# The up products of a gated decoder block: one wide and one narrow matmul per k, and weight sums held behind the up unit's low parts

## The chip, the core and the metric

The kernel runs on one core of one Trainium2 chip. The metric is the time of the program on the device in microseconds (us); lower is better. The engines are TensorE (PE; PEld are its weight loads), VectorE (DVE), ScalarE (ACT), GpSimd (POOL) and SyncE (SP). Each takes its own instructions in the order in which they were built; they meet at semaphores only.

## What is computed

One decoder block on 256 tokens of width 2048, in float32: a mixing half (mLSTM and block attention, merged by gates), then a squared-ReLU MLP with 8192 hidden channels. The change lies in the MLP:

```python
hn = rmsnorm(x, norm_ffn_pre[l])
u = jnp.square(jax.nn.relu(jnp.einsum('bsd,df->bsf', hn, w_up[l])))
y = jnp.einsum('bsf,fd->bsd', u, w_down[l])
x = x + rmsnorm(y, norm_ffn_post[l])
```

## The kernel before

**Products in three parts.** Every float32 operand is split into a high part (rounded to the matmul's input type, by a ScalarE cast, line 167, tiles `whi`) and a low part (what is left, by a VectorE subtraction, line 170, tiles `wlo`). A product is hi x hi + hi x lo + lo x hi. The moving tile of a k holds both parts of the activations side by side, 256 tokens each.

**Two forms of the product by channels.** `mm_feat` (lines 193 and 194), used by the projections, takes two matmuls per k: the high weights against both parts, 512 columns into a whole accumulator, and the low weights against the high part, 256 columns into its first half. `both` (lines 243 and 245) then brings the second half out with a ScalarE copy and adds it to the first on VectorE. `mm_feat_one` (lines 220 to 222) takes three matmuls of 256 columns, all into the first half, and needs no such addition; the up products use it.

**Weight units.** A weight unit is 128 x 2048 (1 MB), loaded by SP into a `raw` tile (3 buffers) or a `rawl` tile (4), and split in two halves of 1024 columns into `whi` and `wlo` (4 buffers each, so two units). An up unit makes 128 of the hidden channels, with 16 k. Its result goes through `up_post`: VectorE takes the maximum with 0 and multiplies by the norm's row factor `rbc` (line 770), ScalarE squares (line 775).

**Chunks.** The MLP runs in 8 chunks of 1024 hidden channels. The down products of chunks 0 to 6 use a seven-product scheme for 2 x 2 blocks in place of eight products. A chunk has two groups p = 0, 1 of seven products, in the order p1, q5, p6, p2, q7, q3, q4. Their weights are the blocks b11, b21, b22 and sums of blocks:

- the weight of q5, `t` = b11 + b12, made on VectorE by the *first sum* (line 879) while b11's unit is prepared; after it, a POOL-queue DMA adds b22 onto b12 (line 880), for q7
- the weight of p6, `t` + b22, made by the *second sum* (line 887) after the split of q5's weight; after the split of that, another POOL-queue DMA adds b21 (line 894), for q4

The activations' factors are sums too (`factors`, lines 787 to 814), made at a chunk's start. Between the down products D of a chunk stand the eight up units U of the next one, as `DUDUDDUDUDDUDUDDUDUDDD`; the second group starts with the eighth D.

**What sets the order.** A loop over the steps emits step i's load and split, then what lies in the list `behind`, then the matmuls and the post of step i - 1. From this program order a scheduler builds each engine's queue; it may move instructions, but `keep_in_program_order` pins those that it is given. A queue does not change at run time. Where L770 stands ahead of a split on VectorE, that split waits until the up unit is done.

Of the kernel before, what the change touches and what calls it, by code (L numbers as in the profile page):

```python
# [19 lines left out]
ALU = mybir.AluOpType  # L20
# [4 lines left out]
T = 256  # L25
# [60 lines left out]
def tile_hybrid_block(ctx, tc, xT, pos, pre, small, wa, wi, wo, wu, wd, wpost, out):  # L86
    nc = tc.nc
    V, S, G, PE = nc.vector, nc.scalar, nc.gpsimd, nc.tensor
# [14 lines left out]
    def t256():  # L103
        return tmp.tile([P, T], F32, name="t256", tag="t256", bufs=6)
# [16 lines left out]
    rbc = const.tile([P, T], F32, name="rbc")  # L121
# [118 lines left out]
    def both(acc):  # L240

        b = t256()
        S.copy(out=b, in_=acc[:, T:2 * T])
        s = t256()
        V.tensor_tensor(out=s, in0=acc[:, 0:T], in1=b, op=ALU.add)
        return s
# [295 lines left out]
    def feat_step(src, mov, post, after_k=None, tail=0, product=mm_feat):  # L542
        st = {}

        def mm(units):
            st["a"] = [acc_tile() for _ in units]
            product(st["a"], units, mov, after_k=after_k, tail=tail)
        steps.append((src if isinstance(src, list) else [src], mm, lambda: post(*st["a"])))
# [217 lines left out]
    uh, xs, todo, behind = {}, {}, [], []  # L766

    def up_post(j, i, acc):
        r = t256()
        V.scalar_tensor_tensor(out=r, in0=acc[:, 0:T], scalar=0.0, in1=rbc, op0=ALU.max,  # L770
                               op1=ALU.mult)
        c = i // 4
        if i % 4 == 0:
            uh[c] = pool["f"].tile([P, 4, T], F32, name="u", tag="u", bufs=2)
        S.activation(out=uh[c][:, i % 4], in_=r, func=AF.Square)
        if j < NCH - 1 and i == 7:
            todo.extend(factors(j))
            for _ in range(2):
                todo.pop(0)()
        elif j == NCH - 1 and i % 4 == 3:  # L780
            for h in range(2):
                factor((j, c, h), uh[c][:, :, h * P:(h + 1) * P])
# [75 lines left out]
    def group(j, p):  # L858
# [5 lines left out]
        r, acc = {}, {}  # L864
# [10 lines left out]
        def w_b11():  # L875
            r["11"], r["12"], r["t"] = load(b11), long_raw(), long_raw()
            nc.sync.dma_start(out=r["12"], in_=b12)
            parts = split(r["11"])
            V.tensor_tensor(out=r["t"], in0=r["11"], in1=r["12"], op=ALU.add)
            nc.gpsimd.dma_start(out=r["12"], in_=b22, accum_op=ALU.add)  # L880
            return [parts]

        def w_t1():
            r["22"] = long_raw()
            nc.sync.dma_start(out=r["22"], in_=b22)
            parts = split(r["t"])
            V.tensor_tensor(out=r["t"], in0=r["t"], in1=r["22"], op=ALU.add)
            return [parts]

        def w_t2():  # L890
# [138 lines left out]
        steps.append(([wd[8 * j + 6], wd[8 * j + 7]], mm, post))  # L1029

    def up_step(j, i):
        feat_step(wu[8 * j + i], hmov, lambda a: up_post(j, i, a), product=mm_feat_one)

    def down_group(j, p):

# [2 lines left out]
        def part(n, what):  # L1038
            def f(*a):
# [8 lines left out]

    feat_step([wu[c] for c in range(4)], hmov, first_up, after_k=x1_squares, tail=4,
              product=mm_feat_one)
    for i in range(4, 8):
        up_step(0, i)
    for j in range(NCH - 1):
# [38 lines left out]
    for i in range(len(steps) + 1):  # L1094
        if i < len(steps) and i not in units:
            src = steps[i][0]
            if i < 4:
                if i == 3:
                    nc.sync.dma_start(out=sm_in, in_=small)
                raws[i] = raw_tile()  # L1100
                start_load(i, raws[i])
                units[i] = [split(raws.pop(i), pieces=2,
                                   between=lambda q, i=i: split_x(4 * i + q))]
            elif callable(src):
                units[i] = src()
            elif len(src) < 4:
                place = places[i]() if i in places else None
                units[i] = [split(load(s), place, half=s.shape[1] // 2, pinned=i in places)
                            for s in src]
            else:  # L1110

                extra = [split(load(s), p.tile([P, 2, 2, 1024], F32R, name=n, tag=n))
                         for s, p, n in ((src[2], pool["mg"], "wu2"), (src[3], pa, "hm"))]
                units[i] = [split(load(src[0]))]

                raw1 = load(src[1])
                late["square"]()
                u1 = [split_half(raw1, 0, pinned=True)]
                late["then"] = lambda: u1.append(split_half(raw1, 1, pinned=True))
                run_step(i - 1)  # L1120
                units[i] += [u1] + extra
                residual()

                raw = load(steps[i + 1][0][0])
                units[i + 1] = [[split_half(raw, 0)]]
                late["then"] = lambda: units[i + 1][0].append(split_half(raw, 1, pinned=True))
                run_step(i)
                continue
            while behind:
                behind.pop(0)()  # L1130
        if i and i - 1 in units:
            run_step(i - 1)
# [71 lines left out]
```

## Time and profile before

| | |
|---|---|
| median of 3 runs | 1424.61 us (1424.54 to 1424.98) |
| profiled execution: its time / its span | 1423.46 / 1421.7 us |
| TensorE busy | 1407.6 us, 99% |
| VectorE busy | 1106.7 us, 78% |
| ScalarE busy | 813.9 us, 57% |
| granted TensorE clock, mean | 0.998 of full speed |

The profile was taken from one execution. Busy time of TensorE is modelled at its ends, since matmuls overlap: the distance from one start to the next tells how fast they run. A row "x2" stands for two instructions merged; "idle before" and the name behind the arrow say how long the engine waited just before and what ended the wait. The MLP takes the last 700 us of the span.

### The profile page before, as it was taken

Reading aid. Unit: us, or ns where it says so; the run is one execution under the profiler, and the core shown is the slowest. Engines: PE = TensorE matmul, PEld = TensorE weight load, DVE = VectorE, ACT = ScalarE, POOL = GpSimd, SP = SyncE. Lnnn points to the kernel's source line nnn. Section 1 sums busy time; section 2 is a strip of 40 time slices with the busy share of each in tenths; the row PEclk is TensorE's granted clock in tenths of the full one; section 3 lists DMA queues with packets and bytes.
Section 4 is the critical chain, followed back from the end, with each engine's and each line's share of the span. In section 5 each row is a group of like instructions: output and inputs, shape, how many; then the busy total and the mean of one; then the engine's idle time right before and its main releaser. Section 6 shows DMA issues by size and latency. Waiting matters only on the chain.

```text
span 1421.7 us, 21825 instructions
## 1 busy us (share of the span) xinstructions
PE 1407.6 (99%) x8570; PEld 1252.6 (88%) x8570; DVE 1106.7 (78%) x1571; ACT 813.9 (57%) x1200; POOL 29.4 (2%) x45
## 2 busy tenths in 40 slices
PE   9999999999999999999999999999999999999997
PEld 7888888888888888888899989989889899988885
DVE  7777766777676666665687888898888989889985
ACT  7655555565554454455656666565655655666561
POOL 0000000000000000000000000000000000000000
PEclk9999999999999999999999999999999999999999
DMA  8654444455445555555618776878768778776761
GB/s 261 221 184 175 159 175 184 177 184 178 178 178 180 192 192 179 191 193 178 238 62 296 250 224 235 269 239 289 232 193 290 234 244 263 239 233 240 242 232 60
DMA packets 46471, 297.13 MB, mean 209 GB/s; under 512 B 5340, under 2 KB 7648, under 8 KB 11936
## 3 DMA queue, kind: packets, MB, share of 16 engines
q1 hardware_dynamic: 41904, 265.57, 49.9%
q0 software_dynamic: 4320, 30.15, 11.4%
q8 instruction: 67, 1.10, 0.3%
q14 instruction: 36, 0.29, 0.1%
q10 hardware_dynamic: 144, 0.01, 0.0%
HBM read 293.61 MB, written 2.10 MB: 208 GB/s over the span
## 4 chain that ended last, share of the span: by engine, by line
PE 96%; DVE 1%; DMA 1%; ACT 0%; issue 0%; SPq 0%; DVEq 0%; ACTq 0%
PE acc L193 27%; PE acc L194 14%; PE acc L222 9%; PE acc L221 9%; PE acc L220 9%; PE acc L231 6%; PE acc L237 6%; PE acc L235 6%; PE acc L205 2%; PE acc L210 2%; PE acc L209 2%; PE sm L231 1%; PE sm L237 1%; PE sm L235 1%; DMA raw<-in_wa_dram 1%; DVE wlo L170 1%
## 5 line engine op out<-in xcount | busy, mean ns | idle before, releaser
L170 DVE TENSOR_TENSOR wlo<-raw,whi 128x1024 fp32r<-128x1024 f32 (+2 forms) x420 | 493.5, 1183 | 218.8 <-ACT whi L167 208.9
L167 ACT CAST whi<-raw 128x1024 fp32r<-128x1024 f32 (+2 forms) x420 | 424.9, 1017 | 406.2 <-PE acc L193 173.8
L193 PE MATMUL acc<-xw,whi 128*128 128x512 f32 x1152 | 408.4, 395 | 0.0
L194 PE MATMUL acc<-xw,wlo 128*128 128x256 f32 x1152 | 328.6, 285 | 0.0
L222 PE MATMUL acc<-hw,wlo 128*128 128x256 f32 x992 | 279.7, 282 | 1.3 <-DVE wlo L170 1.1
L221 PE MATMUL acc<-hw,whi 128*128 128x256 f32 x992 | 279.4, 282 | 0.0
L220 PE MATMUL acc<-hw,whi 128*128 128x256 f32 x992 | 277.7, 282 | 0.0
L193 PEld LDWEIGHTS acc<-xw,whi 128*128 128x128 f32 x1152 | 216.4, 188 | 48.9 <-issue 0.4
L167 ACT CAST whi<-rawl 128x1024 fp32r<-128x1024 f32 x168 | 173.5, 1047 | 113.1 <-PE acc L221 59.0
L194 PEld LDWEIGHTS acc<-xw,wlo 128*128 128x128 f32 x1152 | 216.6, 188 | 0.9
L170 DVE TENSOR_TENSOR wlo<-rawl,whi 128x1024 fp32r<-128x1024 f32 x168 | 201.3, 1221 | 7.0 <-ACT whi L167 5.4
L222 PEld LDWEIGHTS acc<-hw,wlo 128*128 128x128 f32 x992 | 187.1, 189 | 5.3 <-DVE wlo L170 2.9
L220 PEld LDWEIGHTS acc<-hw,whi 128*128 128x128 f32 x992 | 185.9, 188 | 4.2
L221 PEld LDWEIGHTS acc<-hw,whi 128*128 128x128 f32 x992 | 186.8, 188 | 2.1
L231 PE MATMUL acc<-whi,xs 128*128 128x512 f32 x356 | 141.0, 396 | 0.0
L235 PE MATMUL acc<-whi,xs 128*128 128x512 f32 x356 | 140.8, 395 | 0.0
L237 PE MATMUL acc<-wlo,xs 128*128 128x512 f32 x356 | 138.8, 395 | 0.0
L193 PE MATMUL acc<-mg,whi 128*128 128x512 f32 x240 | 84.2, 393 | 0.0
L235 PEld LDWEIGHTS acc<-whi,xs 128*128 128x128 f32 x356 | 66.9, 188 | 14.6
L231 PEld LDWEIGHTS acc<-whi,xs 128*128 128x128 f32 x356 | 66.8, 188 | 13.9 <-ACT whi L167 1.4
L237 PEld LDWEIGHTS acc<-wlo,xs 128*128 128x128 f32 x356 | 66.9, 188 | 13.9
L194 PE MATMUL acc<-mg,wlo 128*128 128x256 f32 x240 | 67.7, 283 | 0.0
(266 smaller groups left out, 1732.3 us busy)
## 6 DMA issues: line engine op xcount, KB each, us to landing
raw<-in_wi_dram SPq DMA_DIRECT2D x96, 1024.0 KB, 4.8
raw<-in_wu_dram SPq DMA_DIRECT2D x64, 1024.0 KB, 7.4
rawl<-in_wd_dram SPq DMA_DIRECT2D x42, 1024.0 KB, 8.9
rawl<-in_wd_dram POOLq DMA_DIRECT2D x28, 1024.0 KB, 9.3
raw<-in_wd_dram SPq DMA_DIRECT2D x22, 1024.0 KB, 7.1
raw<-in_wo_dram SPq DMA_DIRECT2D x16, 1024.0 KB, 4.8
raw<-in_wa_dram SPq DMA_DIRECT2D x8, 520.0 KB, 5.0
raw<-in_wa_dram SPq DMA_DIRECT2D x16, 256.0 KB, 5.2
```

The costliest lines, as they stand in the source:

```text
L167: first = S.copy(out=hi[:, s], in_=r)
L170: second = V.tensor_tensor(out=lo[:, s], in0=r, in1=hi[:, s].bitcast(F32), op=ALU.subtract)
L193: PE.matmul(out=accs[i][:, 0:2 * T], lhsT=hi, rhs=m, start=k == 0, stop=False)
L194: PE.matmul(out=accs[i][:, 0:T], lhsT=lo, rhs=m[:, 0, :], start=False, stop=k == nk - 1)
L205: first = PE.matmul(out=acc, lhsT=m[:, 0, ts], rhs=hi, start=start and k == 0, stop=False)
L209: PE.matmul(out=acc, lhsT=m[:, 1, ts], rhs=hi, start=False, stop=False)
L220: PE.matmul(out=acc, lhsT=hi, rhs=m[:, 0, :], start=k == 0, stop=False)
L221: PE.matmul(out=acc, lhsT=hi, rhs=m[:, 1, :], start=False, stop=False)
L222: PE.matmul(out=acc, lhsT=lo, rhs=m[:, 0, :], start=False, stop=k == KT - 1)
L231: first = PE.matmul(out=acc, lhsT=f[:, k, 0], rhs=hi, start=start and k == 0, stop=False, skip_group_check=more)
L235: PE.matmul(out=acc, lhsT=f[:, k, 1], rhs=hi, start=False, stop=False, skip_group_check=more)
L237: PE.matmul(out=acc, lhsT=f[:, k, 0], rhs=lo, start=False, stop=stop and k == 3, skip_group_check=more)
```

## The change

The up products take `mm_feat`, and `up_post` gets its sum from `both`. Both sums of a group become pinned. The first one, with its DMA, goes into `behind`, so that it is emitted after the next step's split; the second does so in the first group and stays where it was in the second. `behind` is emptied only of what was in it before the step's own load and split.

```diff
     def up_post(j, i, acc):
-        r = t256()
-        V.scalar_tensor_tensor(out=r, in0=acc[:, 0:T], scalar=0.0, in1=rbc, op0=ALU.max,
-                               op1=ALU.mult)
+        r = both(acc)
+        V.scalar_tensor_tensor(out=r, in0=r, scalar=0.0, in1=rbc, op0=ALU.max, op1=ALU.mult)
...
             parts = split(r["11"])
-            V.tensor_tensor(out=r["t"], in0=r["11"], in1=r["12"], op=ALU.add)
-            nc.gpsimd.dma_start(out=r["12"], in_=b22, accum_op=ALU.add)
+
+            def sums():
+                tc.keep_in_program_order(
+                    V.tensor_tensor(out=r["t"], in0=r["11"], in1=r["12"], op=ALU.add))
+                nc.gpsimd.dma_start(out=r["12"], in_=b22, accum_op=ALU.add)
+            behind.append(sums)
             return [parts]
...
             parts = split(r["t"])
-            V.tensor_tensor(out=r["t"], in0=r["t"], in1=r["22"], op=ALU.add)
+
+            def add_22():
+                tc.keep_in_program_order(
+                    V.tensor_tensor(out=r["t"], in0=r["t"], in1=r["22"], op=ALU.add))
+
+            if p == 0:
+                behind.append(add_22)
+            else:
+                add_22()
             return [parts]
...
-        feat_step(wu[8 * j + i], hmov, lambda a: up_post(j, i, a), product=mm_feat_one)
+        feat_step(wu[8 * j + i], hmov, lambda a: up_post(j, i, a))
...
-    feat_step([wu[c] for c in range(4)], hmov, first_up, after_k=x1_squares, tail=4,
-              product=mm_feat_one)
+    feat_step([wu[c] for c in range(4)], hmov, first_up, after_k=x1_squares, tail=4)
...
             src = steps[i][0]
+            waiting = len(behind)
...
-            while behind:
+            for _ in range(waiting):
                 behind.pop(0)()
```

Line numbers behind the edit move: the first sum is line 881 after the change, the second 893, the addition of the halves stays at 245 and the multiply-max at 770.

VectorE's queue in the second group of a chunk, before: the splits of q5's weight (`wlo_10031`, `wlo_10035`), the second sum (L887), the up unit's L770, then the splits of p6's weight (`wlo_10094`, `wlo_10098`).

```order
L170 TENSOR_TENSOR wlo_10031<-rawl_9941,whi_10030 128x1024
L170 TENSOR_TENSOR wlo_10035<-rawl_9941,whi_10034 128x1024
L787 TENSOR_TENSOR xs_10282<-u_9614,xs_10282 128x4x128
L887 TENSOR_TENSOR rawl_9941<-rawl_9941,rawl_10028 128x2048
L770 SCALAR_TENSOR_TENSOR t256_10088<-acc_10039,rbc_90 128x256
L170 TENSOR_TENSOR wlo_10094<-rawl_9941,whi_10093 128x1024
L170 TENSOR_TENSOR wlo_10098<-rawl_9941,whi_10097 128x1024
```

The same place after the change, a chunk of the same kind: the first sum (L881), the splits of q5's weight (`wlo_9654`, `wlo_9658`), the addition of the halves of the up unit that runs between p1 and q5 (L245 on `acc_9662`), the second sum (L893), and the splits of p6's weight (`wlo_9704`, `wlo_9708`).

```order
L881 TENSOR_TENSOR rawl_9577<-raw_9574,rawl_9576 128x2048
L245 TENSOR_TENSOR t256_9622<-acc_9587,t256_9620 128x256
L786 TENSOR_TENSOR xs_9866<-u_9288,xs_9866 128x4x128
L770 SCALAR_TENSOR_TENSOR t256_9622<-t256_9622,rbc_90 128x256
L170 TENSOR_TENSOR wlo_9654<-rawl_9577,whi_9653 128x1024
L170 TENSOR_TENSOR wlo_9658<-rawl_9577,whi_9657 128x1024
L245 TENSOR_TENSOR t256_9697<-acc_9662,t256_9695 128x256
L893 TENSOR_TENSOR rawl_9577<-rawl_9577,rawl_9651 128x2048
L770 SCALAR_TENSOR_TENSOR t256_9697<-t256_9697,rbc_90 128x256
L870 TENSOR_TENSOR y_7422<-y_7422,acc_9712 128x512
L170 TENSOR_TENSOR wlo_9704<-rawl_9577,whi_9703 128x1024
L170 TENSOR_TENSOR wlo_9708<-rawl_9577,whi_9707 128x1024
```

L245 of that up unit now stands ahead of the second sum, where L770 stood behind it; so it does in all seven chunks.

VectorE's queue at the end of a chunk and the start of the next, before: the first sum of the new chunk (L879) stands ahead of the last two products' splits (`wlo_10291` to `wlo_10317`).

```order
L170 TENSOR_TENSOR wlo_10223<-rawl_9940,whi_10222 128x1024
L170 TENSOR_TENSOR wlo_10227<-rawl_9940,whi_10226 128x1024
L879 TENSOR_TENSOR rawl_10341<-raw_10338,rawl_10340 128x2048
L170 TENSOR_TENSOR wlo_10291<-rawl_10028,whi_10290 128x1024
L770 SCALAR_TENSOR_TENSOR t256_10279<-acc_10230,rbc_90 128x256
L170 TENSOR_TENSOR wlo_10295<-rawl_10028,whi_10294 128x1024
L170 TENSOR_TENSOR wlo_10313<-rawl_9941,whi_10312 128x1024
L801 TENSOR_TENSOR s_a_10285<-u_9614,u_10004 128x512
L943 TENSOR_TENSOR y_7486<-y_7486,acc_10298 128x512
L170 TENSOR_TENSOR wlo_10317<-rawl_9941,whi_10316 128x1024
```

Further on in the same queue, before: the splits of the new chunk's first up unit (its second half, `wlo_10376`), of q5's weight, of the second up unit (`wlo_10466`, `wlo_10470`) around the second sum (L887).

```order
L170 TENSOR_TENSOR wlo_10376<-raw_10369,whi_10375 128x1024
L810 TENSOR_TENSOR u_9614<-u_9614 128x4x128
L170 TENSOR_TENSOR wlo_10398<-rawl_10341,whi_10397 128x1024
L170 TENSOR_TENSOR wlo_10402<-rawl_10341,whi_10401 128x1024
L170 TENSOR_TENSOR wlo_10466<-raw_10463,whi_10465 128x1024
L787 TENSOR_TENSOR xs_10380<-u_9614,xs_10380 128x4x128
L770 SCALAR_TENSOR_TENSOR t256_10459<-acc_10410,rbc_90 128x256
L887 TENSOR_TENSOR rawl_10341<-rawl_10341,rawl_10395 128x2048
L814 TENSOR_TENSOR s_b_10320<-s_b_10320,u_10004 128x512
L170 TENSOR_TENSOR wlo_10470<-raw_10463,whi_10469 128x1024
```

The same stretch after the change: the splits of the first up unit (`wlo_9954`, `wlo_9958`), the first sum (L881), the factors, the splits of q5's weight, of the second up unit (`wlo_10036`, `wlo_10040`), and the second sum (L893).

```order
L170 TENSOR_TENSOR wlo_9954<-raw_9951,whi_9953 128x1024
L805 TENSOR_TENSOR s_b_9904<-s_a_9869,u_9288 128x512
L870 TENSOR_TENSOR y_7422<-y_7422,acc_9882 128x512
L786 TENSOR_TENSOR xs_9871<-s_a_9869,xs_9871 128x4x128
L170 TENSOR_TENSOR wlo_9958<-raw_9951,whi_9957 128x1024
L881 TENSOR_TENSOR rawl_9925<-raw_9922,rawl_9924 128x2048
L809 TENSOR_TENSOR u_9288<-u_9288 128x4x128
L786 TENSOR_TENSOR xs_9906<-s_b_9904,xs_9906 128x4x128
L786 TENSOR_TENSOR xs_9935<-u_9625,xs_9935 128x4x128
L170 TENSOR_TENSOR wlo_9982<-rawl_9925,whi_9981 128x1024
L170 TENSOR_TENSOR wlo_9986<-rawl_9925,whi_9985 128x1024
L813 TENSOR_TENSOR s_b_9904<-s_b_9904,u_9625 128x512
L170 TENSOR_TENSOR wlo_10036<-raw_10033,whi_10035 128x1024
L170 TENSOR_TENSOR wlo_10040<-raw_10033,whi_10039 128x1024
```

The first sum moved from ahead of the old chunk's last products to behind the new chunk's first up unit, and the second sum from between the halves of the second up unit to behind both.

## Rows read from the trace of the kernel before

**Rows 1.** The page: busy time by engine, and the chain that ended last.

```profile
PE 1407.6 (99%) x8570; PEld 1252.6 (88%) x8570; DVE 1106.7 (78%) x1571; ACT 813.9 (57%) x1200; POOL 29.4 (2%) x45
...
PE 96%; DVE 1%; DMA 1%; ACT 0%; issue 0%; SPq 0%; DVEq 0%; ACTq 0%
```

**Rows 2.** Busy time of each engine, by chunk of the MLP.

```profile
core 0: us, PE busy (x) PEld busy (x) DVE busy (x) ACT busy (x) POOL busy (x), PEclk, DMA share, GB/s
894.34:979.46 85.12, 85.12 (x553) 77.21 (x553) 75.93 (x78) 51.33 (x60) 3.45 (x4) 1.00 0.78 249
979.46:1065.22 85.76, 85.38 (x553) 77.08 (x553) 75.39 (x77) 50.99 (x59) 3.44 (x4) 1.00 0.75 244
1065.22:1150.38 85.16, 85.16 (x553) 77.25 (x553) 75.75 (x78) 51.37 (x60) 3.45 (x4) 1.00 0.77 249
...
1235.55:1322.50 86.95, 85.76 (x553) 77.04 (x553) 76.43 (x79) 51.53 (x60) 3.45 (x4) 1.00 0.74 240
```

**Rows 3.** TensorE in order of time (start us, us, engine, line), single matmuls.

```profile
990.41 0.28 PE L220 MATMUL acc<-hw,whi 128*128 128x256 f32 x1
990.53 0.28 PE L221 MATMUL acc<-hw,whi 128*128 128x256 f32 x1
...
995.99 0.28 PE L222 MATMUL acc<-hw,wlo 128*128 128x256 f32 x1
996.11 0.40 PE L231 MATMUL acc<-whi,xs 128*128 128x512 f32 x1
...
999.39 0.39 PE L237 MATMUL acc<-wlo,xs 128*128 128x512 f32 x1
...
1047.91 0.28 PE L222 MATMUL acc<-hw,wlo 128*128 128x256 f32 x1
```

**Rows 4.** Output projection's narrow matmul: count, minimum/median/maximum ns, first and last start us.

```profile
L194 PE MATMUL acc<-mg,wlo x240: 279/283/285, 621.6 to 705.5; 128*128 128x256 f32 x120
```

**Rows 5.** Groups by line: count | busy us, mean ns | idle before, releaser.

```profile
L245 DVE TENSOR_TENSOR t<-acc,t 128x256 f32<-128x256 f32 x119 | 49.1, 417 | 0.0
L243 ACT COPY t<-acc 128x256 f32<-128x256 f32 x119 | 42.7, 364 | 0.0
L879 DVE TENSOR_TENSOR rawl<-raw,rawl 128x2048 f32<-128x2048 f32 x14 | 32.1, 2293 | 13.9 <-DMA raw<-in_wd_dram 11.8 <-DMA rawl<-in_wd_dram 2.0
L887 DVE TENSOR_TENSOR rawl<-rawl 128x2048 f32<-128x2048 f32 x14 | 32.0, 2284 | 0.0
```

**Rows 6.** VectorE, then TensorE, in order of time, at an old stall.

```profile
1056.30 2.29 DVE L879 TENSOR_TENSOR rawl<-raw,rawl 128x2048 f32<-128x2048 f32 x1 [2.31 <-DMA raw<-in_wd_dram]
...
1059.78 0.39 PE L222 MATMUL acc<-hw,wlo 128*128 128x256 f32 x1 [0.38 <-DVE wlo L170]
```

**Rows 7.** VectorE in order of time, second group, around the second sum (L887).

```profile
993.26 2.28 DVE L887 TENSOR_TENSOR rawl<-rawl 128x2048 f32<-128x2048 f32 x1
996.31 0.42 DVE L770 SCALAR_TENSOR_TENSOR t<-acc,rbc 128x256 f32<-128x256 f32 x1 [0.77 <-PE acc L222]
996.74 2.36 DVE L170 TENSOR_TENSOR wlo<-rawl,whi 128x1024 fp32r<-128x1024 f32 x2
```

**Rows 8.** ScalarE in order of time, the casts that follow that sum.

```profile
995.66 2.00 ACT L167 CAST whi<-rawl 128x1024 fp32r<-128x1024 f32 x2 [3.65 <-DVE rawl L887]
```

**Rows 9.** VectorE in order of time, a chunk's start: its first and last rows.

```profile
1013.84 2.29 DVE L879 TENSOR_TENSOR rawl<-raw,rawl 128x2048 f32<-128x2048 f32 x1 [0.42 <-DMA rawl<-in_wd_dram]
1016.05 1.22 DVE L170 TENSOR_TENSOR wlo<-rawl,whi 128x1024 fp32r<-128x1024 f32 x1
...
1035.21 2.28 DVE L887 TENSOR_TENSOR rawl<-rawl 128x2048 f32<-128x2048 f32 x1
...
1045.83 2.36 DVE L170 TENSOR_TENSOR wlo<-raw,whi 128x1024 fp32r<-128x1024 f32 x2
...
1051.68 1.23 DVE L170 TENSOR_TENSOR wlo<-raw,whi 128x1024 fp32r<-128x1024 f32 x1 [0.63 <-ACT whi L167]
```


## The prediction

> **What bounds the kernel now.** I read the busy line and the chain of waits first: TensorE is busy 1407.6 of 1421.7 us and the chain that ended last lies on it for 96% [rows 1]. So only two things move the time: how long TensorE needs per matmul, and whether its operands are there. Next come the chunks of the MLP, from one chunk's start to the next: they last 85.12 to 86.95 us, TensorE is full in them, and VectorE is busy 75 to 76 us of each [rows 2]. ScalarE has more room (51 us). VectorE is therefore the second limit. Being busy for 89% it has room on average, but it takes its instructions in order, so the question is where in a chunk it has room. For that I set the times of its rows against the time at which TensorE starts on the low half of each weight unit (L222 and L237 read it). The order of the built program says what stands ahead of what after the change; every time below is from the rows of before.
>
> **Part 1, the up products.** Three matmuls of 256 columns per k become one of 512 and one of 256. Price of the old form: an up unit of 48 matmuls starts at 990.41 and its successor at 996.11, 5.70/16 = 0.356 us per k; two starts in a row lie 0.12 apart, which gives 0.360 [rows 3]. Price of the new form: the output projection runs it already, 240 pairs from 621.6 to 705.5, 83.9/239 = 0.351 [rows 4]. The gain per k is 0.005 to 0.009 us, times 1024 (64 units of 16) 5.3 to 9.2 us; I take 6.4, near the end that the longer row gives. Here a rule of the Trainium skill speaks against the size: its page "TensorE: Matmul & The Clock Gate", section "Back-to-back issue gap", gives an isolated matmul its columns at 2.4 GHz and some 2.5 ns. An estimate by that page is 2.5 ns for each matmul that goes, 2.6 us in all, so 3.8 us less gain. The rows show 5 ns or more, and they decide.
>
> **Part 2, the halves added on the way out.** Each of the 64 up units gains a ScalarE copy (0.364) and a VectorE add (0.417) [rows 5], 23.3 and 26.7 us in sum; the multiply-max on L770 stays, on SBUF instead of PSUM. On ScalarE I price it at nothing: it idles 34 us of a chunk. On VectorE it is 8 x 0.36 (the rows overlap by some 0.06) = 2.9 us per chunk, of 9 us of room, so what it costs hangs on the place. The first four units' adds stand while VectorE would wait anyway, and I price them at nothing.
>
> **Part 3, the sums moved.** Each chunk has two groups of seven down products, and each group two sums of whole weight units, 2.29 and 2.28 us [rows 5], now meant to stand behind the next up unit's low halves. That takes away today's small stalls: at 1056.30 the first sum waited 2.31 us for a load, the low half behind it came late, and TensorE idled before 1059.78 [rows 6]. Over the chunks the stalls are what two chunks exceed the shortest by, 0.64 and 1.83, so 2.5 us of gain [rows 2]. The DMAs that follow each sum on the POOL queue move with it; they are asked for four or five steps later, so I price that at nothing (a landing takes some 9 us, a step 2.8 or 5.7).
>
> Now the two places where the new order costs.
>
> *Second group, second sum.* The add of b22 is not held there. Its result is the weight of the third product (L237 reads it from 999.39). Before, it ran at 993.26, while TensorE was in the up unit, ahead of L770, which waits for that unit's end and starts at 996.31; the low half ran from 996.74 to 997.96, so 1.43 us were to spare [rows 3, 7]. The cast follows the sum by 0.1 us and lasts some 1.0 [rows 8]. After, the new add L245 of that same up unit stands ahead of the sum in VectorE's queue, in all seven chunks, and L245 waits for the unit's end and the ScalarE copy. So: release 996.31, copy to 996.67, add to 997.09, sum to 999.4, cast to 1000.4, low half to 1001.65, against 999.39: TensorE waits 2.3 us. Bounds: 2.0 (the release at the last start, 995.99) and 2.6 (a cast late by the 0.3 of a wait's end). Seven chunks: 16.1 us (14 to 18).
>
> *First group, the start of a chunk.* From 1016.05 to the wait before 1051.68 VectorE has no idle time but works 35 us through: the factors of the new chunk and the last products of the old fall together [rows 9]. Here it is the bound, and TensorE runs on what VectorE has ahead: the low half for the third up unit runs at 1045.83 for about 1.2 (the row holds two), and TensorE takes it at 1047.91, some 0.86 later [rows 3, 9]. Before, the first sum stood outside, at 1013.84, put where VectorE waited anyway. After, it is pinned behind the first up unit's low halves, in the middle of the stretch: 2.2 us more, and three adds of 0.36 come on top, 3.3 us. Less the 0.86 to spare that is 2.4, and TensorE comes 0.3 us earlier after three faster units, so it waits 2.7 us. Bounds: 1.7 (the adds find gaps) and 3.6 (nothing to spare). The first chunk has no old products to finish, so this happens in six: 16.2 us (10 to 22). The second up unit, which the old second sum made late, gains its slack back, but the products behind it do not: the work ahead of them is the same plus 3.3.
>
> **The sum**, against the profiled execution (span 1421.7, its own time 1423.46; the median of the runs is 1424.61, 1.15 above): -6.4 - 2.5 + 16.1 + 16.2 = +23.4. From the median that is 1448.0.
>
> **Rivals.**
> *Only one of the two places costs.* For it: the 0.86 us is the slack of one row, and the scheduler also moved other products of the stretch, so VectorE may enter it with more done. Against: the buffers hold two units, so it can't get far ahead. Then -8.9 + 16.1: 1431.8.
> *Faster: the sums land in room.* This needs the b22 sum to be done by 998.1, so that cast and low half end before TensorE needs them; it decides at L245: if the unit's end didn't hold the queue there, the 1.43 us to spare would stay. And VectorE's 9 us of room per chunk would have to be had at the chunk's start, too. For it: room on average, and projections that run the same adds at a full TensorE. Against: the order, which is fixed when the kernel is built. Then only the gains: 1415.7.
> *The change does less than it says*, only in this: the b22 sum of the second group is not held, and stands behind a longer wait than before. That is inside the forecast.
> *Worse: the copy blocks everywhere.* ScalarE takes it in order, so casts behind it wait for TensorE's unit end at each of the eight units of a chunk. If each product behind an up unit lost the copy's 0.36 us, 64 x 0.36 = 23 us come on top: 1471. Against: the casts have 2.8 us until TensorE asks for them.
>
> **How the numbers follow.** Forecast (both places) 0.62, at 1448.0; one place 0.17, 1431.8; faster 0.11, 1415.7; worse everywhere 0.08, 1471; gains and waits that cancel 0.02. The range holds the forecast with its bounds (1424.6 - 9.2 - 2.5 + 14 + 10 = 1437 to 1424.6 - 5.3 - 2.5 + 18 + 22 = 1457) and the second case: 1431 to 1458, leaving out some 0.2. A measurement of this kernel tells 0.2%, about 3 us, from no change. Faster 0.11, same 0.02, slower 0.87.
>
> **What would show it.** Right: in the profile after, per chunk, an idle stretch of TensorE of about 2.3 us at the third product of the second group, ended by ScalarE's cast or VectorE's low half, with the b22 sum starting behind L245 and after the up unit's end; some 2.7 us of waits for low halves in the first 40 us of a chunk, VectorE without gaps there; chunks of about 89 us; up units of 5.62 us. Wrong: chunks near 84.5 us and the b22 sum running inside the up unit; or VectorE idle at the chunk's start; or up units still at 5.70.

## The result and the profile after

The changed kernel takes 1455.2 us (median of 4 runs, 1454.32 to 1457.23) against 1424.6 (1422.74 to 1424.98) of the kernel before in the same comparison: a ratio of 1.0221, interval [1.0209, 1.0234]. That is 30.6 us slower; 23.4 were forecast. The profiled execution has a span of 1452.2 us.

The page's busy line and its chain of waits, which answer to [rows 1]:

```profile
PE 1415.2 (97%) x7546; PEld 1202.9 (83%) x7546; DVE 1123.8 (77%) x1635; ACT 832.1 (57%) x1264; POOL 29.4 (2%) x45
...
PE 85%; DVE 10%; issue 2%; ACT 2%; DMA 1%; SPq 0%; DVEq 0%; ACTq 0%
```

TensorE runs 1024 matmuls fewer, and VectorE has taken 10% of the chain where it had 1%. The chunks of the MLP (busy us of each engine, with the granted clock after POOL), against [rows 2]:

```profile
core 0: us, PE busy (x) PEld busy (x) DVE busy (x) ACT busy (x) POOL busy (x), PEclk, DMA share, GB/s
866.50:955.84 89.34, 86.38 (x430) 70.98 (x428) 77.58 (x86) 53.15 (x68) 3.43 (x4) 1.00 0.74 235
955.84:1045.23 89.39, 85.98 (x425) 70.33 (x424) 77.70 (x87) 53.38 (x68) 3.44 (x4) 1.00 0.75 235
...
1134.60:1225.52 90.92, 87.50 (x425) 71.53 (x424) 77.80 (x87) 53.47 (x68) 3.44 (x4) 0.98 0.74 232
1191.00:1194.00 3.00, 3.00 (x9) 2.37 (x8) 3.00 (x4) 1.96 (x4) 0.87 (x1) 0.52 0.82 131
```

A chunk lasts 89.4 us where it lasted 85.1 to 87.0, and VectorE is busy only some 2 us more in it. One chunk is longer still, 90.92; the last row, a stretch inside it, shows why: a granted clock of 0.52, close to the lower of TensorE's two levels, 1.2 instead of 2.4 GHz. Two more such stretches of 3.4 us stand at 832 and 1372 us.

**The second group's third product.** VectorE, ScalarE and TensorE in order of time; before in [rows 3, 7, 8]:

```profile
1000.01 2.28 DVE L881 TENSOR_TENSOR rawl<-raw,rawl 128x2048 f32<-128x2048 f32 x1
...
1003.48 2.35 DVE L170 TENSOR_TENSOR wlo<-rawl,whi 128x1024 fp32r<-128x1024 f32 x2
1006.24 0.42 DVE L245 TENSOR_TENSOR t<-acc,t 128x256 f32<-128x256 f32 x1 [0.41 <-ACT t L243]
1006.59 2.28 DVE L893 TENSOR_TENSOR rawl<-rawl 128x2048 f32<-128x2048 f32 x1
...
1008.96 1.99 ACT L167 CAST whi<-rawl 128x1024 fp32r<-128x1024 f32 x2 [2.75 <-DVE rawl L893]
...
1010.05 0.50 PE L231 MATMUL acc<-whi,xs 128*128 128x512 f32 x1 [1.44 <-ACT whi L167]
...
1011.32 0.50 PE L237 MATMUL acc<-wlo,xs 128*128 128x512 f32 x1 [0.54 <-DVE wlo L170]
```

The last five rows are the chain of the forecast: add of halves, second sum, cast, and TensorE that waits for it. The first two, the held first sum and q5's low halves, matter below. Measured by its starts beyond the usual spacing, TensorE loses 1.61 and 0.69 us there: 2.3 in five of the seven chunks, 2.5 in the first and 2.7 in the last.

**The start of a chunk**, VectorE, ScalarE and TensorE, against [rows 9]:

```profile
951.83 2.29 DVE L881 TENSOR_TENSOR rawl<-raw,rawl 128x2048 f32<-128x2048 f32 x1
...
955.84 2.36 DVE L170 TENSOR_TENSOR wlo<-rawl,whi 128x1024 fp32r<-128x1024 f32 x2
...
954.21 2.00 ACT L167 CAST whi<-rawl 128x1024 fp32r<-128x1024 f32 x2 [3.45 <-DVE rawl L881]
...
955.64 0.40 PE L235 MATMUL acc<-whi,xs 128*128 128x512 f32 x1
957.12 0.50 PE L237 MATMUL acc<-wlo,xs 128*128 128x512 f32 x1 [1.08 <-DVE wlo L170]
```

VectorE works from 941 to 975 us without idle time, the held first sum in the middle. TensorE waits for a low half of q5's weight, which is that sum itself: sum, cast and, behind three instructions of the factors, the low half. By starts this wait costs 1.24 us in four of the six chunks. With shorter ones, the longest 0.43 us at a cast that stands behind those of the held second sum, it makes some 2.7 us per chunk.

TensorE's waits over the MLP (us in total, times, longest us):

```profile
PE acc L231 <- ACT whi L167: 13.0, 13, 1.7
PE acc L237 <- DVE wlo L170: 8.2, 11, 1.1
PE acc L231 <- ACT xs L785: 2.0, 1, 2.0
```

The third is a single wait that the forecast did not have, at 778 us, at the start of the first chunk.

### The profile page after: what moved, and what is told of

Its sections match the earlier page's. It is cut to its first block, busy times and chain, and to the rows that moved or that the text cites. A ratio compares the mean times of both kernels' runs of the same rounds, so it can differ in the third digit from the quotient of the medians.

```text
span 1452.2 us, 19922 instructions
## 1 busy us (share of the span) xinstructions
PE 1415.2 (97%) x7546; PEld 1202.9 (83%) x7546; DVE 1123.8 (77%) x1635; ACT 832.1 (57%) x1264; POOL 29.4 (2%) x45
## 4 chain that ended last, share of the span: by engine, by line
PE 85%; DVE 10%; issue 2%; ACT 2%; DMA 1%; SPq 0%; DVEq 0%; ACTq 0%
PE acc L193 39%; PE acc L194 20%; PE acc L237 5%; PE acc L231 5%; PE acc L235 5%; DVE wlo L170 4%; DVE rawl L893 2%; PE acc L210 1%; PE acc L205 1%; PE acc L209 1%; ACT whi L167 1%; DVE rawl L881 1%; PE sm L237 1%; DMA raw<-in_wa_dram 1%; PE sm L231 1%
## 5 line engine op out<-in xcount | busy, mean ns | idle before, releaser
L193 PE MATMUL acc<-hw,whi 128*128 128x512 f32 x992 | 355.7, 395 | 1.2 <-ACT whi L167 1.2
L170 DVE TENSOR_TENSOR wlo<-rawl,whi 128x1024 fp32r<-128x1024 f32 x168 | 202.0, 1222 | 37.4 <-ACT whi L167 36.9
L193 PEld LDWEIGHTS acc<-hw,whi 128*128 128x128 f32 x992 | 186.9, 188 | 44.3 <-ACT whi L167 1.6
L231 PE MATMUL acc<-whi,xs 128*128 128x512 f32 x356 | 144.0, 405 | 15.0 <-ACT whi L167 13.0
L237 PE MATMUL acc<-wlo,xs 128*128 128x512 f32 x356 | 142.4, 404 | 8.5 <-DVE wlo L170 8.2
L235 PE MATMUL acc<-whi,xs 128*128 128x512 f32 x356 | 142.3, 400 | 0.0
L245 DVE TENSOR_TENSOR t<-acc,t 128x256 f32<-128x256 f32 x183 | 75.9, 418 | 3.3 <-ACT t L243 2.5
L243 ACT COPY t<-acc 128x256 f32<-128x256 f32 x183 | 66.0, 364 | 13.3 <-PE acc L194 13.3
```

What stands on the lines that cost most here:

```text
L170: second = V.tensor_tensor(out=lo[:, s], in0=r, in1=hi[:, s].bitcast(F32), op=ALU.subtract)
L193: PE.matmul(out=accs[i][:, 0:2 * T], lhsT=hi, rhs=m, start=k == 0, stop=False)
L231: first = PE.matmul(out=acc, lhsT=f[:, k, 0], rhs=hi, start=start and k == 0, stop=False, skip_group_check=more)
L235: PE.matmul(out=acc, lhsT=f[:, k, 1], rhs=hi, start=False, stop=False, skip_group_check=more)
L237: PE.matmul(out=acc, lhsT=f[:, k, 0], rhs=lo, start=False, stop=stop and k == 3, skip_group_check=more)
```

## The experiments

The kernel before ran beside every group of runs, at 1423.3 to 1424.2 us. To set runs side by side I also use one figure worked out from each trace: from 745 to 1400 us, each distance from a matmul's start to the next, less the median distance of matmuls of that shape, summed where it exceeds 20 ns. This lost time of TensorE is 4.1 us before and 41.5 after. Less the 5.8 us that the shorter up units give (below), 37.4 more is 31.6 us, and the runs show 30.6.

| kernel | us | ratio to before, interval | lost time of TensorE |
|---|---|---|---|
| changed kernel | 1455.2 | 1.0221 [1.0209, 1.0234] | 41.5 |
| products alone | 1428.2 | 1.0038 [1.0023, 1.0053] | 17.6 |
| sums alone | 1454.5 | 1.0216 [1.0199, 1.0233] | 35.3 |
| second sum ahead of the add | 1452.7 | 1.0203 [1.0188, 1.0219] | 39.7 |
| first group's sums as before | 1445.9 | 1.0156 [1.0138, 1.0173] | 31.8 |
| second group's sums as before | 1448.1 | 1.0172 [1.0155, 1.0189] | 32.6 |
| changed, wait filled | 1452.3 | 1.0199 [1.0184, 1.0214] | 34.4 and the fill |
| first group's as before, wait filled | 1438.8 | 1.0110 [1.0095, 1.0126] | 20.4 and the fill |
| products alone, no halves added | 1419.2 | 0.9965 [0.9952, 0.9978] | 5.7 |
| products alone, maximum on GpSimd | 1447.2 | 1.0161 [1.0141, 1.0181] | 33.7 |
| first group's as before, a unit between | 1430.8 | 1.0053 [1.0039, 1.0067] | 17.6 |
| first group's as before, spread | 1419.0 | 0.9961 [0.9948, 0.9975] | 5.7 |
| changed, spread | 1431.7 | 1.0053 [1.0039, 1.0066] | 19.2 |

**1. Each half of the change alone.** The products alone keep the sums as they were:

```diff
-            def sums():
-                tc.keep_in_program_order(
-                    V.tensor_tensor(out=r["t"], in0=r["11"], in1=r["12"], op=ALU.add))
...
-            behind.append(sums)
+            V.tensor_tensor(out=r["t"], in0=r["11"], in1=r["12"], op=ALU.add)
+            nc.gpsimd.dma_start(out=r["12"], in_=b22, accum_op=ALU.add)
```

> The up products of the changed kernel (one wide and one narrow matmul per k, halves added on the way out) with both weight sums where they were before. Theory (the waits come from where the sums stand): the second group's second sum stands ahead of L245 again, so its 2.5 us per chunk are gone; at a chunk's start only three adds of 0.36 come on top, 1.1 less 0.86 to spare, so some 0.5 us in six chunks. 1424.6 - 6.4 + 3 = 1421 us (1418 to 1424). Rival (copies and adds themselves cost, at every up unit): 64 x 0.36 on top, 1440 us or more.

The sums alone keep the three narrow matmuls (`product=mm_feat_one`, no `both`):

> Only the sums moved as in the change; the up products stay three narrow matmuls with no addition of halves. Theory: L770 now stands ahead of the second group's second sum as L245 did, without the copy: about 1.9 us in seven chunks, 13 us; at a chunk's start 2.2 us more less 0.86 to spare, 1.4 in six, 8 us; the first chunk's factors some 2; the old stalls go, -2.5. 1424.6 + 20 = 1445 us (1438 to 1449). Rival (the adds are what fills VectorE, the place of the sums doesn't matter): 1422 to 1425 us.

Neither came out as expected. The products alone lost some 5 us instead of winning 3.6, the sums alone lost 31, all of the change's loss, where 20 were expected. In the trace of the sums alone the third product loses the 1.9 us expected, a chunk's start 2.3 instead of 1.4, and three stretches at half clock come on top, which the expectation had not priced. The two do not add: 5 and 31 are 36, the change costs 30.6. VectorE and TensorE of the products alone, where the second group's first sum waits for its load, with the group row of that sum (idle before it: 22.0 us in all; before the change 13.9 [rows 5]):

```profile
972.67 2.29 DVE L878 TENSOR_TENSOR rawl<-raw,rawl 128x2048 f32<-128x2048 f32 x1 [3.19 <-DMA raw<-in_wd_dram]
974.88 1.22 DVE L170 TENSOR_TENSOR wlo<-raw,whi 128x1024 fp32r<-128x1024 f32 x1
...
976.15 0.38 PE L194 MATMUL acc<-hw,wlo 128*128 128x256 f32 x1 [0.59 <-DVE wlo L170]
...
L878 DVE TENSOR_TENSOR rawl<-raw,rawl 128x2048 f32<-128x2048 f32 x14 | 32.1, 2290 | 22.0 <-DMA raw<-in_wd_dram 21.6 <-DMA rawl<-in_wd_dram 0.5
```

The sum stands ahead of the up unit's low half and holds it up while it waits. This is the old stall of [rows 6], grown: holding the sum removes it, and that is what the other half of the change buys.

**2. The cause of the wait at the third product.** The forecast blamed the add of halves that stands ahead of the second sum. Here the add is pinned, so that the sum stands ahead of it:

```diff
-        V.tensor_tensor(out=s, in0=acc[:, 0:T], in1=b, op=ALU.add)
+        add = V.tensor_tensor(out=s, in0=acc[:, 0:T], in1=b, op=ALU.add)
+        if pinned:
+            tc.keep_in_program_order(add)
...
-        r = both(acc)
+        r = both(acc, True)
```

> The changed kernel with the up units' addition L245 pinned too, so that the second group's second sum keeps its place ahead of the L245 of the up unit that runs before it (six of seven chunks had it behind, or all). Nothing else is edited. Theory: the 2.5 us at the third product of the second group go in seven chunks, 17.6 us, and with them the three stretches at half clock that follow this wait, some 5 us: 1455.2 - 22.6 = 1432.6 us (1430 to 1437). Rival (VectorE is full over the whole chunk, so a wait removed here comes back elsewhere): 1450 us or more.

1452.7: the theory fell. VectorE at the same place, the first sum (L883 here), the low halves made from it, and the second sum (L895), and then TensorE:

```profile
1001.21 2.28 DVE L883 TENSOR_TENSOR rawl<-raw,rawl 128x2048 f32<-128x2048 f32 x1
...
1004.68 2.35 DVE L170 TENSOR_TENSOR wlo<-rawl,whi 128x1024 fp32r<-128x1024 f32 x2
1007.07 2.29 DVE L895 TENSOR_TENSOR rawl<-rawl 128x2048 f32<-128x2048 f32 x1
...
1010.55 0.50 PE L231 MATMUL acc<-whi,xs 128*128 128x512 f32 x1 [0.73 <-ACT whi L167]
```

The rows are one chain: the held first sum, its cast on ScalarE (three short instructions run on VectorE meanwhile), its low halves, the second sum, its cast. From the first sum's start to the product it takes 9.3 us with the add out of the way; in the changed kernel it took 10.0 (1000.01 to 1010.05). The add was worth 0.45 of the 2.3 us (the waits fell to 0.89 and 0.95).

**3. One group's sums at a time.** First the first group's as before, the second's held as in the changed kernel, then the other way round; the same edit with `p == 1` and `p == 0`:

```diff
-                tc.keep_in_program_order(
-                    V.tensor_tensor(out=r["t"], in0=r["11"], in1=r["12"], op=ALU.add))
+                made = V.tensor_tensor(out=r["t"], in0=r["11"], in1=r["12"], op=ALU.add)
+                if p == 1:
+                    tc.keep_in_program_order(made)
...
-            behind.append(sums)
+            if p == 1:
+                behind.append(sums)
+            else:
+                sums()
```

> The changed kernel with the first group's two sums issued and left unpinned as before; the second group's sums as in the change. Theory: the waits at a chunk's start go, 2.7 us in six chunks, and the first chunk's 2.2: 1455.2 - 18.4 = 1437 us (1433 to 1441), with the 2.3 us wait of the second group still there in every chunk. Rival (the start of the chunk is bound by VectorE whatever the order, since the adds fill it): above 1450 us.

> The changed kernel with the weight sums of the second group where they were before (made at once, not pinned) and those of the first group held and pinned as in the changed kernel. Theory (the held first sum of the second group is what makes its second sum late and the products wait 2.5 us in each of 7 chunks, and the half clock follows from those waits): 1455.2 - 17.5 - 5 = 1432.7, the waits at the first group's start stay, and no half clock after the second group's third product. Rival (most of the loss is in the first group, or the second group's sums wait elsewhere when they are not held, as in the kernel with the products alone): 1444, which is the kernel with the products alone, 1428.2, and the 16 us of the first group.

With the first group free the waits at the chunk's start fall from 16.5 us over the MLP to 3, and the first chunk's from 2.2 to 1.1. Yet only 9 us of the expected 18 come back: the half clock now follows the wait at the third product in six of seven chunks, three stretches more than in the changed kernel. A stretch of 3.4 us holds eight starts 0.43 us apart, which take 1.9 us at 0.233, so it costs some 1.5 us (the expectations put it at 1.7): 13.5 + 1.1 - 4.6 = 10.0, and 9.3 were measured. With the second group free the wait at its third product is gone in six of seven chunks (1.6 us in the last), and so is the half clock there. In that kernel, as in experiment 2, the second sum stands ahead of the add (1002.46 and 1005.64 us), but its first sum is early: so it is the held first sum that makes most of the wait. But the time is 1448.1, nearer to the rival: its first sum waits for its load again and holds up the up unit's low halves. The group row of the first sums in that kernel:

```profile
L880 DVE TENSOR_TENSOR rawl<-raw,rawl 128x2048 f32<-128x2048 f32 x14 | 32.0, 2289 | 25.1 <-DMA raw<-in_wd_dram 25.1
```

So in this order of steps, with the halves' adds on VectorE, the second group's first sum costs in either place: early it waits for its load, late it makes the second sum late.

**4. The half clock.** Four matmuls with zero weights, into the same bank, in the wait ahead of the third product:

```diff
                     acc[bank] = late[bank, p]
+                    if bank == "p6" and p == 1 and j > 0:
+                        for q in range(4):
+                            tc.keep_in_program_order(PE.matmul(
+                                out=acc[bank], lhsT=zero[:, 0:1].to_broadcast([P, P]),
+                                rhs=hmov(q), start=False, stop=False, skip_group_check=True))
```

> The changed kernel, with four extra matmuls of 512 columns ahead of the second group's third product in all chunks but the first; their weights are zeros, so they add nothing to the bank. The orders of VectorE and ScalarE are those of the changed kernel. They stand in the wait of 1.44 us there and last about 4 x 0.23 = 0.9 us, so they cost nothing by themselves. Theory (the granted clock falls to 0.5 after TensorE has idled in that wait): no stretch at half clock at the two later places of the three where the changed kernel had one (about 1191 and 1372 us), the first chunk's (about 833 us), which is not filled, may stay; 2 x 1.7 us less, 1451.8. Rival (the half clock has another cause, or the fill is not what counts): the stretches stay, 1455 or, if the fill delays the product, up to 1460.

> The kernel with the first group's sums as before and the second group's held (1445.9), with four matmuls of 512 columns on zero weights ahead of the second group's third product in all chunks but the first, in its wait. Without them the half clock followed the wait in 6 of the 7 chunks. Theory (the clock falls because TensorE idles there): no half clock in the six filled chunks, 6 x 1.7 = 10 us less, 1436; the idle time before the product falls by about 0.9 us and the product starts no later. Rival (the fill changes nothing in the clock, or the earlier run had none by chance): four or more stretches at half clock, 1444 to 1448.

1452.3 and 1438.8. In both no filled chunk has half clock: none of six where the changed kernel had it in two of these six, none of six where the kernel without the fill had it in all six. In both the unfilled first chunk has it at this wait; the first run's profile has one more at 779 us, after the wait of 2.16 us that stands there in the changed kernel too. Two stretches of 5 us behind the third product, of the kernel without the fill and then with it (same columns as the chunks, the granted clock after POOL):

```profile
917.00:922.00 5.00, 4.49 (x13) 3.58 (x14) 5.00 (x5) 3.60 (x6) 0.87 (x1) 0.66 0.86 149
1006.00:1011.00 5.00, 4.50 (x13) 3.60 (x14) 4.99 (x5) 3.61 (x6) 0.87 (x1) 0.66 0.78 138
```

```profile
919.00:924.00 5.00, 4.28 (x19) 3.28 (x20) 4.84 (x5) 5.00 (x7) 0.87 (x1) 1.00 0.91 175
1006.50:1011.50 5.00, 4.33 (x19) 3.32 (x20) 4.88 (x5) 5.00 (x7) 0.87 (x1) 1.00 0.89 182
```

In five microseconds 19 matmuls start where 13 did. The fill itself and the product behind it:

```profile
1005.04 1.08 PE L931 MATMUL acc<-hw,zero 128*128 128x512 f32 x4
1006.64 0.50 PE L234 MATMUL acc<-whi,xs 128*128 128x512 f32 x1 [0.52 <-ACT whi L170]
```

The product waits for its cast as before; only the idle time ahead of it is shorter. So TensorE's idling there is what takes the clock down. All runs of the second kernel agree: their mean granted clock is 0.989 to 0.993 without the fill and 0.995 to 0.998 with it. The second run's gain, 7.1 us, is six stretches less one that this profile has in the first chunk, 5 x 1.55 = 7.7, within the runs' scatter.

**5. Where the products' gain goes.** The products alone, with copy and add left out of the 64 up units:

```diff
-        r = both(acc)
-        V.scalar_tensor_tensor(out=r, in0=r, scalar=0.0, in1=rbc, op0=ALU.max, op1=ALU.mult)
+        r = t256()
+        V.scalar_tensor_tensor(out=r, in0=acc[:, 0:T], scalar=0.0, in1=rbc, op0=ALU.max,
+                               op1=ALU.mult)
```

> The kernel with the products alone (wide and narrow matmuls, weight sums as before) with the copy and the add of the halves left out of the 64 up units: the multiply-max reads the first half of the bank alone, so the products of the activations' low parts are dropped from the result. Theory (the matmuls do give the 6 us, and the 0.42 us of VectorE and 0.36 us of ScalarE per unit take them and more away, by pushing the weights' low halves back): 1424.6 - 6.4 = 1418, bounds 1416 to 1420. Rival (the wide and narrow pair gives little in the up units, or the load on VectorE does not matter): 1426 to 1428.

1419.2: the theory's figure. The matmuls do win 5 us, and copy and add together take 9 away, all of it as waits: lost time 5.7 against 17.6, where the 17.6 is of a profiled execution of 1431.6 us, 3.4 above the median, with a stretch at half clock at 1151 us. Which of the two, copy or add, takes how much is not shown. To take as much from VectorE in another way, the maximum and the row factor went to GpSimd:

```diff
-        V.scalar_tensor_tensor(out=r, in0=r, scalar=0.0, in1=rbc, op0=ALU.max, op1=ALU.mult)
+        G.tensor_scalar(out=r, in0=r, scalar1=0.0, scalar2=None, op0=ALU.max)
+        G.tensor_tensor(out=r, in0=r, in1=rbc, op=ALU.mult)
```

> The kernel with the products alone (wide and narrow matmuls, weight sums as before, 1428.2) with the multiply-max of each up unit taken from VectorE, now that its input lies in SBUF, and done by two GpSimd instructions (max, multiply). VectorE loses 0.36 us x 8 = 2.9 us of work per chunk, about what the halves' adds brought (3.3 us). Theory (VectorE's load is what the products' gain is lost to): most of the waits go, 1418 to 1422, faster than the kernel before. Rival (the longer chain copy, add, two GpSimd steps, square makes the last unit's activations late for the factors, or GpSimd slows VectorE on the SBUF): 1428 to 1436.

1447.2, worse than either. A ScalarE row and GpSimd's group row for the multiply (64 times, mean 1602 ns; the maximum has 1557) show one half of the rival; the group row of VectorE's low halves in this kernel and, last, in the products alone show the other:

```profile
1056.04 0.42 ACT L775 ACTIVATE u<-t 128x256 f32<-128x256 f32 x1 [3.82 <-POOL t L771]
...
L771 POOL TENSOR_TENSOR t<-t,rbc 128x256 f32<-128x256 f32 x64 | 102.5, 1602 | 8.4 <-ACT rbc L300 3.4
...
L170 DVE TENSOR_TENSOR wlo<-rawl,whi 128x1024 fp32r<-128x1024 f32 x168 | 214.5, 1304 | 28.6 <-ACT whi L167 28.6
...
L170 DVE TENSOR_TENSOR wlo<-rawl,whi 128x1024 fp32r<-128x1024 f32 x168 | 203.1, 1218 | 8.8 <-ACT whi L167 8.3
```

ScalarE's square waits 3.82 us for GpSimd, with the next casts behind it in its queue. And VectorE did not get lighter: in the MLP the low halves that run beside a GpSimd instruction take 1375 ns on average, up to 1768, the others 1218, so that VectorE is busy 1129.8 us in this kernel and 1122.8 in the products alone. So this run does not tell what a lighter VectorE would bring, nor how the loss divides between the two halves of the rival.

**6. Another order of the steps.** If the chain of two sums is too long for one product, an up unit between second and third product must cover it. The kernel with the first group's sums as before, and one step moved in the second group:

```diff
-        for what in "DUDUDDUDUDDUDUDDUDUDDD":
+        for what in "DUDUDDUDUDDUDUDUDDUDDD":
```

> The kernel with the first group's sums as before and the second group's held (1445.9), with the order of the steps in a chunk changed: in the second group an up unit stands between the second and the third product, as it already does in the first group (U D1 U D2 U D3 D4 U D5 D6 D7 instead of U D1 U D2 D3 U D4 U D5 D6 D7); as many steps as before. Theory (second and third product next to each other make first sum, cast, low halves, second sum, cast, low half one serial chain that is longer than one product; a unit of 5.6 us between them covers it, and without the wait the clock stays up): 1445.9 - 7 x 2.3 - 6 x 1.7 = 1419.6, faster than the kernel before (1424.2). Rival (VectorE is simply too full, the wait moves to another step of the group): 1428 to 1446, with waits of 1 us and more at the second group's fourth or fifth product.

1430.8: the wait at the third product is gone, and no stretch at half clock is left before the program's end, but 15 of the expected 26 us came. The next waits stand around the row of four products (three of a chunk, one of the next). TensorE's largest entry there (total, times, longest):

```profile
PE sm L231 <- ACT whi L167: 4.8, 5, 1.5
```

So the products were spread, three in a row at most. This is run with the first group's sums as before and, second, with the changed kernel's own sums:

```diff
-        for what in "DUDUDDUDUDDUDUDDUDUDDD":
+        for what in "DUDUDDUDDUDDUDUDDUDUDD":
```

> The kernel with the first group's sums as before and the second group's held, with the 14 products of a chunk spread more evenly between its 8 up units: D U D U DD U DD U DD U D U DD U D U DD, so that second and third product are apart in both groups (as in the run with a unit between them, 1430.8) and at most three products stand in a row, two of a chunk and the first of the next, where there were four. What is left in the run with a unit between them are waits of 0.5, 0.56 and 1.0 us around that row of four in three of seven chunks and 1.0 to 1.6 us in two more. Theory (those waits are VectorE falling behind over the row of four products, which each need 2.4 us of low halves in 1.9 us): 1419 to 1423, faster than the kernel before (1423.3) or level with it. Rival (two products, 3.7 us, after the last unit are too short for copy, add, max, square, difference and split of the factors): new waits of 1 to 2 us at the first product of each chunk, 1431 to 1440.

> The changed kernel with the same more even order of steps (D U D U DD U DD U DD U D U DD U D U DD). Theory (the wait at the second group's third product needs the second and third product next to each other, the half clock needs that wait, and the waits at the first group's start come from the row of four products with held sums on top): 1455.2 - 17.6 - 5 = 1432.6 with the waits at the start unchanged, about 1425 with half of them gone. Rival (holding the sums costs as much in any order): 1445 to 1455.

(The expectation of the first speaks of 1.9 us per product. That is wrong: twelve starts 0.233 apart are 2.8 us, and two products are 5.6. What stands is the comparison: two low halves, 2.35, and the add into `y`, 0.6, are 3.0 us of VectorE for a product of 2.8, and it falls behind in a row of them.)

The first takes 1419.0 us and beats the kernel before by 5 us. Two chunks of it, and TensorE's largest waits over the MLP:

```profile
854.37:938.81 84.44, 84.27 (x425) 70.80 (x424) 76.29 (x85) 53.92 (x70) 3.43 (x4) 1.00 0.78 251
938.81:1023.26 84.45, 84.27 (x426) 70.78 (x424) 77.01 (x86) 52.99 (x67) 3.45 (x4) 1.00 0.76 243
```

```profile
PE acc L231 <- ACT whi L167: 1.0, 6, 0.2
PE acc L194 <- DVE wlo L170: 0.9, 1, 0.9
```

A chunk is 84.45 us with 77 us of VectorE in it, as much as in the changed kernel's 89.4. The same adds, copies and sums cost nothing there: 1419.0 is what the kernel without the halves' adds takes. The second, 1431.7, has the figure of the theory, 1432.6: 23.5 us of the 30.6 came from the places, not from the work. In part that is luck: the theory left the waits at the start unchanged, but the 1.24 us at q5 are gone, though its sum is still held, and 1.32 us at the fourth product came (2.4 us per chunk in all). What it still loses lies with the first group's held sums. ScalarE and TensorE at that group's third and fourth product, whose matmuls alternate there:

```profile
957.86 3.89 ACT L167 CAST whi<-rawl 128x1024 fp32r<-128x1024 f32 x4 [4.11 <-DVE rawl L893]
...
960.85 0.49 PE L231 MATMUL acc<-whi,xs 128*128 128x512 f32 x1 [1.17 <-ACT whi L167]
```

Four casts in a row wait 4.11 us for the second sum, and the third of them is what TensorE needs.

## Why the prediction was right, and where it was not

**Direction and the two places: right, in the sum.** Slower, by waits of TensorE at the third product of the second group and at the start of a chunk, in the sizes forecast: 2.3 us (forecast 2.3) and some 2.7 us (2.7) per chunk. Chunks are 89.4 us; "about 89" stood under what would show it. VectorE has no gaps at the chunk's start, as forecast, and undoing the sums of the first group alone takes nearly all of those waits away. The row is another, though. The forecast let VectorE's load delay the third up unit's low half; its largest part, 1.24 us, stands earlier, at q5, whose weight is the held first sum, and at the third up unit itself none is left. The load has its share: with the products spread, VectorE gets to that sum in time, and the 1.24 us are gone.

**Part 1: right in the trace.** An up unit now takes 5.61 us, from its first start to the next step's:

```profile
1022.17 0.40 PE L193 MATMUL acc<-hw,whi 128*128 128x512 f32 x1
...
1027.78 0.40 PE L231 MATMUL acc<-whi,xs 128*128 128x512 f32 x1
```

Against 5.70 that is 0.09 x 64 = 5.8 us (forecast 6.4), and 5.6 ns for each matmul that goes. The Trainium skill's page "TensorE: Matmul & The Clock Gate", section "Back-to-back issue gap", gives 2.5 ns, by estimate 2.6 us in all; the measurement differs, and it decides.

**The cause at the third product: wrong, with the right size.** The step that failed is "L245 of that same up unit stands ahead of the sum". It does, and costs 0.45 us. The step took the second sum of before, 993.26, as ready to run early and only held by the queue. But what it adds to is the first sum, and that was now held too: the sum could not have run early in any order. The forecast looked at what stands ahead of an instruction and not at when its operand is made. That the size agreed is luck: with the add the wait is 2.3 us, and with the add out of the way 1.84 are left; only the experiments tell the two chains apart.

**Missed: the first chunk.** 2.16 us at 778: the first sum, pinned, stands ahead of the last up unit's add, and with it of the first factors. The forecast gave the first chunk no loss. With the first group's sums as before it is gone, and 1.11 us for an up unit's low half stand there, as in the products alone.

**Missed: the half clock.** Three stretches of some 1.55 us, 4.6 in all. The forecast priced a wait at its own length. With both terms added, 23.4 + 2.2 + 4.6 = 30.2, and 30.6 were measured.

**Part 2: right for this kernel only.** The forecast priced copy and add at what they cost at the chunk's start. In the kernel with the products alone they cost 9 us, most plainly at a place that the forecast had not looked at, the second group's first sum with its load; the changed kernel hides that by holding the sum. The gain of 2.5 us for the old stalls was therefore a gain on a stall that the new products would have made larger.

**The rivals.** Faster fell with the result. One place only fell: with the held sums of either group alone the kernel is still 22 and 24 us above the kernel before. The copy that blocks everywhere did not show: ScalarE is the releaser at the third product, and there because of the sum.

**Open.** Why the half clock follows the same wait in two of six later chunks of the changed kernel and in all six with the first group free. The wait of 2.16 us at 778 to 780 us is of the same kind: five of the profiles have it, and the half clock follows it in four, not in the changed kernel's. Whether the kernel before, with its narrow products, would gain from the spread order: this was not run.

## What to carry to other kernels

When an instruction moves, follow its operands back as well as the queue ahead of it; two steps that are each held behind the same work can form one serial chain, and then the order behind them matters little (0.45 of 2.3 us here). Work added to an engine with 10% of room can cost nothing or 9 us, by where its steps stand: spreading the steps gave back 23.5 and 26.9 us, leaving out the copies and adds 9.0. And price a wait of TensorE with what the clock does after it.

## What the runs showed of the hardware

I had not expected the granted clock to fall to 0.5 after waits of about 2 us in a program that keeps TensorE busy 97% of its span; before the change it stays at 1.00 in the MLP [rows 2] until 1414.6 us, at the program's end. Matmuls of 512 columns then start 0.43 us apart, not 0.233, for 3.4 us, so each such stretch costs some 1.5 us beside the wait. Zero-weight matmuls in the wait kept the clock at 1.00 in 12 of 12 places, in two profiles. The Trainium skill's page "TensorE: Matmul & The Clock Gate", section "A second HAM failure mode: psum-queue depth-cycling", says of another kernel that frequent short idles between groups of matmuls let the clock swing between its levels; the row with 0.52 and the rows with 0.66 agree with it.

GpSimd took 1.56 and 1.60 us (means) for an operation on 128 x 256 float32 for which VectorE needs 0.42, and up to 6.3 us for a single one; the time of one of its instructions could not be read from one row. VectorE's subtraction of a low half, beside it, took 1375 ns on average instead of 1218.
